# Decoder block on one core: two products of the fourth column pair ahead of the second input half's sums

## The chip, the core and the metric

The kernel runs on 1 core of one Trainium2 chip. The metric is the device time of one execution in microseconds (us). Before the change the median of 3 runs is 2165.49 us (2165.3 to 2165.86). All times of instructions below come from one profiled execution of the same kernel.

## The reference

One decoder layer, in float32, on x of shape (1, 1024 tokens, 1024 features): a gated token mixer, then a squared-ReLU MLP, then a final RMSNorm. The change lies in the first product of the MLP.

```python
h = modulate(rms_norm(x, norm2_g[l]), sh2, sc2)
x = x + g2[:, None, :] * squared_relu_mlp(h, w_ff1[l], w_ff2[l])

def squared_relu_mlp(h, w1, w2):
    return jnp.square(jax.nn.relu(h @ w1)) @ w2      # w1: 1024 x 4096, w2: 4096 x 1024
```

## The kernel before

Activations lie transposed: 8 tiles of 128 features by 1024 tokens. Every float32 operand is split into a high part (a cast on ACT, the scalar engine) and a low part (source minus high part, a subtraction on DVE, the vector engine), and each 128x128 by 128x512 step on PE, the tensor engine, is three matmuls (`mm3`, L210, L212, L214: low weight, low input, high by high).

`ff1` (L2404) computes h @ w1 by a scheme with seven block products in place of eight. The 4096 columns of w1 go in 16 pairs q = 0 to 15 of 2 x 128 columns. The inputs are cut into feature tiles of even and odd number (four of each) and into two halves of 512 tokens. A product is named (q, n); n says which input and weight blocks it takes:

- "11" and "12" take the first token half as it is (`h2h`, `h2l`, split before `ff1` begins) and the pair's weight blocks as they are ("unsummed");
- "s1", "s3", "s2" take sums of input blocks t1, t3, t2 (tiles `xt10h` to `xt13l`, and `xt30`, `xt20` and so on, high and low half of one tile), and weight sums, made on DVE in `fs` by `prep` (L240);
- "s4" takes the second half's odd tiles (`x220h` to `x223l`), "22" the sum t4.

Each product is four steps of `mm3`, 12 matmuls. `prep` makes a product's weights: DVE adds (`fs`, L252, for sums), ACT casts the high part (L257), DVE subtracts for the low part one `prep` later (`flush`, L267). The weight tiles come from a list of slots; the last three tiles called wh and three called wl come back to the list when the product that reads them has been written (`mm`, L281). `post` (L284) takes results out of PSUM: after "11" a copy on ACT (`ft0nsq`, L289); after "s2" two DVE operations (`ft0nsq` L295, `ft0h2t` L296) and one more (`a`, L2360); "22" accumulates on the bank that `ft..h2t` has read, so it has to wait for it. ACT then applies ReLU and the square (L2361, L2362), and `a_sums` (L2377 to L2382) makes the sums that the second MLP product needs.

The order on each engine is the order of the code (`tc.manual_schedule()`); waits between engines are semaphores. At the start of `ff1` the second token half isn't normalised yet: DVE scales its eight tiles (`norm`, L2410), makes t1 (L2432), t3 (L2449), t2 (L2458), t4 (L2475), and ACT and DVE split each sum (`x_split`, L2398 and L2399; L2401 and L2402 for the odd tiles). PE meanwhile computes (0,11), (1,11), (0,12), (1,12), (2,11), (0,s1), (1,s1), (2,12), (0,s3), (1,s3), (0,s2), (1,s2), then the s4 and 22 of pairs 0 and 1, and then pairs 2 to 15 in turn, with (3,11) put between (2,s2) and (2,22). To free its PSUM bank the finished (0,11)+(0,12) is copied aside (L2425, tile `f11`), and later that of pair 2 (L2496).

The raw weights come by `w1_load` (L2326), a DMA of 512 KB on the SP queue, pairs 0 and 1 during the output projection before, pair 2 at its end, pairs 3 and 4 when the input tiles `x1` come free (L2490).

Of the kernel before, what the change touches and what calls it, by code (L numbers as in the profile page):

```python
# [11 lines left out]
F32 = mybir.dt.float32  # L12
# [5 lines left out]
P = 128  # L18
# [122 lines left out]
def block_kernel(ctx, tc, io, stop=None, dbg=None):  # L141
    nc = tc.nc
# [29 lines left out]
    def ps_s(name, shape=(P, 512)):  # L172
        return PS["p"].tile(list(shape), F32, tag="s", bufs=PS["n"], name=name)
# [42 lines left out]
    def wk(w, k):  # L216

        return w[0][:, k * P:(k + 1) * P], w[1][:, k * P:(k + 1) * P]
# [6 lines left out]
    ORDER = ("11", "s1", "s3", "s2", "12", "22", "s4")  # L225
# [3 lines left out]
    class Blocks:  # L229
# [10 lines left out]
        def prep(self, *items):  # L240

            for q, n in items:
                b11, b12 = self.raw[q, 1][:, :512], self.raw[q, 1][:, 512:]
                b21, b22 = self.raw[q, 2][:, :512], self.raw[q, 2][:, 512:]
                if self.low and self.low[:2] == (q, {"s2": "s1", "s4": "s2"}.get(n)):
                    self.flush()
                if n[0] == "s":
                    if n == "s1":
                        self.s[q] = self.sums(f"{self.name}s{q}")
                    src = self.s[q][:, int(n == "s3")]  # L250
                    x, y = {"s1": (b21, b22), "s2": (src, b11), "s3": (b21, b11), "s4": (src, b12)}[n]
                    nc.vector.tensor_add(src, x, y)  # L252
                else:
                    src = {"11": b11, "12": b12, "22": b22}[n]
                kind = self.slots.pop(0)
                t = self.place(kind, f"{self.name}w{q}{n}")
                nc.scalar.copy(t[:, :512], src)  # L257
                self.flush()
                self.low = q, n, t, src
                self.w[q, n] = t, kind  # L260
# [1184 lines left out]
    RGW, n = [], 0  # L1445
# [543 lines left out]
    G = {}  # L1989
# [187 lines left out]
    def r_split(blk, p):  # L2177
        i, hf = 2 * p + int(blk[0]) - 1, int(blk[1]) - 1
        m = G[1, i][:, 512 * hf:512 * hf + 512]
        if blk == "21":  # L2180
            t = A["r1"].tile([P, S], F32R, tag="att", bufs=8, name=f"m{i}{hf}")
            hi, lo = t[:, :512], t[:, 512:]
        else:
            hi, lo = mh(f"mh{i}{hf}"), mh(f"ml{i}{hf}")
        nc.scalar.copy(hi, m)
        nc.vector.tensor_sub(lo, m, fv(hi))
        G["m", i, hf] = hi, lo
# [56 lines left out]
    def norm_acc(x, f, key, pool):  # L2244

        n = x.shape[1]
        if f == 0:
            acc = pool.tile([P, 512], F32, tag="nacc", bufs=2, name=f"acc{key}")[:, :n]
            nc.scalar.activation(acc, x, AF.Square)
            G["acc", key] = acc  # L2250
        else:
            sq = pool.tile([P, 512], F32, tag="nsq", bufs=3, name=f"sq{key}{f}")[:, :n]
            nc.scalar.activation(sq, x, AF.Square)  # L2253
            if key == "nf2" and f == 7:
                G["sq"] = sq
            else:
                (nc.vector if f == 7 else nc.gpsimd).tensor_add(G["acc", key], G["acc", key], sq)  # L2257

    def wo_step(hf, f):
        def body(w):  # L2260
            if hf == 0 and f < 4:
                r_split("12", f)
                r_split("22", f)
            if hf == 0 and 0 < f < 5:
                w1_load((f - 1) % 2, 1 + (f - 1) // 2)
            if (hf, f) in EARLY:
                BF.prep(*EARLY[hf, f])
            if hf == 1 and f in (5, 6):
                w1_load(2, f - 4)
            hs = slice(512 * hf, 512 * hf + 512)  # L2270
            ps = ps_s(f"wo{hf}{f}")
            ks = (0, 2, 4, 6, 1, 3, 5, 7)
            for k in ks:
                mm3([ps], wk(w, k), [G["m", k, hf]], k == 0, k == 7)
            if hf == 1 and f == 0:
                G["rs"] = rstd_rows(G["acc", "n20"], "n20", G["mp"])
            if hf == 1 and f == 1:
                G["rb"] = rstd_bcast(G["rs"], 0, 4, "n20")
            if hf == 1 and 1 < f < 7:
                h2_first(((0, 1), (2,), (3, 4), (5,), (6, 7))[f - 2])  # L2280
            x = G["x1", f][:, hs]
            nc.vector.scalar_tensor_tensor(x, ps, mods[:, G1 + f:G1 + f + 1], x, op0=ALU.mult, op1=ALU.add)
            nc.sync.dma_start(x1_d[f][:, hs], x)
            norm_acc(x, f, f"n2{hf}", G["mp"])
        return body
# [34 lines left out]
    NQ = DFF // 256  # L2320


    NS = 3
    a_d = {t: dram.tile([P, S], F32, name=f"ad{t}") for t in range(8 * NS, 2 * NQ)}
    xs_d = [dram.tile([P, 7, 4, 512], F32, name=f"xsd{c}") for c in range(NS)]
    def w1_load(q, part):  # L2326

        if q < 2:
            t = G["p"].tile([P, 1024], F32, tag="g1", bufs=8, name=f"w1r{q}{part}")
        elif q < 3:  # L2330
            t = wraw.tile([P, 1024], F32, tag="raw", name=f"w1r{q}{part}")
        else:
            t = G["p"].tile([P, 1024], F32, tag="g0", bufs=8, name=f"w1r{q}{part}")
        nc.sync.dma_start(t, io["w_ff1"][2 * q + part - 1])
        BF.raw[q, part] = t
# [10 lines left out]

    def f_temps(name, i):
        t = ("nsq", "h2t")[i]
        return G["mp"].tile([P, 512], F32, tag=t, bufs=3 - i, name=name + t)

    def f_out(q, n, x, y=None):

# [19 lines left out]
    def a_sums(q, part):  # L2372
# [7 lines left out]
        else:  # L2380
# [5 lines left out]
    BF = Blocks("f", X, ["g1"] * 4 + ["att*"] * 4 + ["att"] * 2 + ["att*"] * 2 + ["wh", "wl"] * 3,  # L2386
                lambda kind: kind in ("att", "wh", "wl"), f_place, f_sums, f_temps, f_out)
# [16 lines left out]
    def ff1(ahead):  # L2404
        def t_(k, half):
            return G["x1", k][:, 512 * half:512 * half + 512]
# [14 lines left out]
        BF.prep((2, "s3"), (2, "12"))  # L2421
        BF.mm(0, "12")

        t = G["mp"].tile([P, 512], F32, tag="f11", name="f11")
        nc.scalar.copy(t, BF.ps[0][0])  # L2425
        BF.ps[0][0] = t
        BF.mm(1, "12")
        low = None
        for m in range(4):
            norm(2 * m)  # L2430
# [4 lines left out]
            low = x_split("t1", m, t1, None, "mh", 32)  # L2435
        norm(1)
        low()
        BF.mm(2, "11")
        BF.post(2, "11")
        BF.mm(0, "s1")  # L2440
        BF.mm(1, "s1")
        BF.mm(2, "12")
        lows = []
        for m in range(4):
            if m > 0:
# [6 lines left out]
            low = x_split("t3", m, t3, G["p"], "g1", 8)  # L2452

        def t2(m):
            k = 2 * m + 1
            t = t_(k, 1)
            lows[m]()
            nc.vector.scalar_tensor_tensor(t, t, mods[:, SH2 + k:SH2 + k + 1], t_(2 * m, 0), op0=ALU.add, op1=ALU.add)  # L2458
            return x_split("t2", m, t, G["p"], "g1", 8)

        for m in range(4):
            l = t2(m)
            low()
            low = l
            if m == 0:
                BF.mm(0, "s3")
                BF.mm(1, "s3")
        low()
        BF.mm(0, "s2")
        BF.mm(1, "s2")  # L2470
# [7 lines left out]
        low = t4(0)  # L2478
        BF.post(0, "s2")
        low()  # L2480
        low = t4(1)
        BF.post(1, "s2")
        low()
        low = t4(2)
# [2 lines left out]
        l()  # L2487
        for k in range(NK):
            del G["x1", k]
        for q in (3, 4):  # L2490
            for part in (1, 2):
                w1_load(q, part)
        for q in range(2):
            BF.post(q, "12")
        t = G["mp"].tile([P, 512], F32, tag="f11", name="f11b")
        nc.scalar.copy(t, BF.ps[2][0])  # L2496
        BF.ps[2][0] = t
        sums = [(q, n) for q in range(2, NQ) for n in ORDER if (q, n) not in ((2, "11"), (2, "12"))]
        rest = [(q, n) for q, n in sums if (q, n) != (3, "11")]
        rest.insert(3, (3, "11"))  # L2500
        items = [(q, n) for n in ("s4", "22") for q in range(2)] + rest

        def before(q, n):
            if q > 2 and n == ORDER[0] and q + 2 < NQ:
                for part in (1, 2):
                    w1_load(q + 2, part)
            if q == NQ - 1 and n in ("s2", "12"):
                for f in range(3):
                    x1_load(f + 3 * (n == "12"), x1_d)

        late = {(0, "22"): (0, 0), (2, "s1"): (0, 1), (2, "22"): (1, 0), (2, "s4"): (1, 1), (3, "s1"): (2, 0), (3, "s3"): (2, 1)}
        late.update({(q + 1, n): (q, part) for q in range(3, 4 * NS) for part, n in enumerate(("11", "s1"))})

        def between(q, n):
            if q < 3 and (q, n) in late:
                a_sums(*late[q, n])
            if (q, n) == (2, "22"):
                BF.post(2, "12")
            if (q, n) == (NQ - 1, "22"):
                b_load(1)  # L2520

        def after(q, n):
# [4 lines left out]
            if q == NQ - 1:  # L2527
                second_ahead(n)

        BF.run(items, sums[2:], before, after, lambda q, n: n == "s2" or n == "22" and q < 2,  # L2530
               lambda q: 1 if q == 2 else 9, between)
        b_load(2)
        x1_load(6, x1_d)
        x1_load(7, x1_d)
# [404 lines left out]
```

## Time and profile before

| what | value |
|---|---|
| runs | 2165.3, 2165.49, 2165.86 us |
| the profiled execution's own time | 2165.45 us |
| its span (first to last instruction) | 2163.6 us |
| granted TensorE clock, mean | 0.999 |
| PE busy | 2141.4 us, 99% |
| DVE busy | 1492.1 us, 69% |
| ACT busy | 983.5 us, 45% |
| first and last start of an `ff1` matmul | 1520.1 and 1831.2 us |

A row of the timeline gives the start in us from the span's start, the duration in us, the engine, the line of the kernel, the operation, output and inputs, sizes and count; in brackets the idle time of that engine just before and what ended it. Matmuls overlap: one lasts 0.39 us, and the next starts 0.227 us after it.

### The profile page before, as it was taken

Reading aid. Unit: us, or ns where it says so; the run is one execution under the profiler, and the core shown is the slowest. Engines: PE = TensorE matmul, PEld = TensorE weight load, DVE = VectorE, ACT = ScalarE, POOL = GpSimd, SP = SyncE. Lnnn points to the kernel's source line nnn. Section 1 sums busy time; section 2 is a strip of 40 time slices with the busy share of each in tenths; the row PEclk is TensorE's granted clock in tenths of the full one; section 3 lists DMA queues with packets and bytes.
Section 4 is the critical chain, followed back from the end, with each engine's and each line's share of the span. In section 5 each row is a group of like instructions: output and inputs, shape, how many; then the busy total and the mean of one; then the engine's idle time right before and its main releaser. Section 6 shows DMA issues by size and latency. Waiting matters only on the chain. (4 is left out here: it accounts for less than half of the span.)

```text
span 2163.6 us, 27394 instructions
## 1 busy us (share of the span) xinstructions
PE 2141.4 (99%) x10036; PEld 1782.8 (82%) x10036; DVE 1492.1 (69%) x2320; ACT 983.5 (45%) x1769; POOL 203.2 (9%) x267
## 2 busy tenths in 40 slices
PE   8999999999999999999999999999999999999998
PEld 6888888888888888888888888888778888888887
DVE  6885777777654677666667644777876665977855
ACT  5553322323244566666556635334454455533413
POOL 0001111100001333321110000001000000000003
PEclk9999999999999999999999999999999999999999
DMA  9859998845576655537776366653244435645322
GB/s 383 286 208 301 296 299 248 226 154 202 194 291 241 229 186 180 177 123 213 215 186 188 137 240 221 216 177 129 69 166 161 156 144 195 245 131 175 108 88 78
DMA packets 162931, 425.19 MB, mean 197 GB/s; under 512 B 28261, under 2 KB 56172, under 8 KB 159724
## 3 DMA queue, kind: packets, MB, share of 16 engines
q1 hardware_dynamic: 150456, 374.90, 49.0%
q0 software_dynamic: 9648, 48.24, 10.1%
q8 instruction: 79, 1.29, 0.2%
q10 hardware_dynamic: 2692, 0.30, 0.1%
q14 instruction: 56, 0.46, 0.1%
HBM read 324.13 MB, written 160.32 MB: 224 GB/s over the span
## 5 line engine op out<-in xcount | busy, mean ns | idle before, releaser
L210 PE MATMUL qap<-hh,qaw 128*128 128x512 f32 x264 | 102.7, 389 | 0.0
L212 PE MATMUL qap<-hl,qaw 128*128 128x512 f32 x264 | 102.7, 389 | 0.0
L214 PE MATMUL qap<-hh,qaw 128*128 128x512 f32 x264 | 102.7, 389 | 0.0
L620 POOL TENSOR_TENSOR j<-qk,j 128x512 fp32r<-128x512 f32 x32 | 42.8, 1338 | 400.9 <-ACT j L619 385.5
L2257 POOL TENSOR_TENSOR accnf<-accnf,sqnf 128x256 f32<-128x256 f32 (+1 forms) x18 | 16.6, 923 | 610.0 <-ACT sqnf L2253 610.0
L2361 ACT ACTIVATE a<-a 128x512 f32<-128x512 f32 x48 | 30.3, 631 | 73.7 <-DVE a L2360 73.7
L2569 ACT CAST w2h<-w2s 128x512 fp32r<-128x512 f32 x36 | 22.4, 621 | 78.6 <-DVE w2s L2607 75.7
L214 PEld LDWEIGHTS qap<-hh,qaw 128*128 128x128 f32 x264 | 49.6, 188 | 10.4
L212 PEld LDWEIGHTS qap<-hl,qaw 128*128 128x128 f32 x264 | 49.5, 188 | 10.3
L210 PEld LDWEIGHTS qap<-hh,qaw 128*128 128x128 f32 x264 | 49.5, 188 | 10.3
L267 DVE TENSOR_TENSOR fw<-w1r,fw 128x512 fp32r<-128x512 f32 x48 | 32.9, 688 | 33.6 <-ACT fw L257 33.6
L686 ACT ACTIVATE on<-oT,gnt 128x128 f32<-128x128 f32 x128 | 48.2, 455 | 15.7 <-PE oT L682 15.6
L267 DVE TENSOR_TENSOR qaw<-wa,qaw 128x512 fp32r<-128x512 f32 x66 | 44.0, 686 | 9.6 <-ACT qaw L257 9.6
L2092 DVE TENSOR_TENSOR rwl<-rwl,rwh 128x1024 fp32r<-128x1024 f32 x25 | 30.2, 1220 | 29.1 <-ACT rwh L2122 29.1
L210 PE MATMUL fp<-h2h,fw 128*128 128x512 f32 x128 | 50.0, 390 | 0.0
L1620 ACT ACTIVATE P<-P,ng 128x128 f32<-128x128 f32 (+1 forms) x96 | 41.9, 439 | 17.5 <-DVE ng L1612 17.5
L212 PE MATMUL fp<-h2l,fw 128*128 128x512 f32 x128 | 49.8, 389 | 0.0
L214 PE MATMUL fp<-h2h,fw 128*128 128x512 f32 x128 | 49.8, 389 | 0.0
L210 PE MATMUL roa<-rh,rwl 128*128 128x512 f32 x128 | 49.8, 389 | 0.0
L212 PE MATMUL roa<-rl,rwh 128*128 128x512 f32 x128 | 49.8, 389 | 0.0
L214 PE MATMUL roa<-rh,rwh 128*128 128x512 f32 x128 | 49.8, 389 | 0.0
L656 DVE TENSOR_TENSOR sm<-sm,sT 128x128 f32<-128x128 f32 x32 | 9.2, 288 | 54.6 <-ACT sm L655 54.6
(3092 smaller groups left out, 7214.2 us busy)
## 6 DMA issues: line engine op xcount, KB each, us to landing
v<-vd SPq DMA_DIRECT2D x32, 512.0 KB, 5.1
w1r<-in_w_ff_dram SPq DMA_DIRECT2D x32, 512.0 KB, 4.6
yt<-y POOLq DMA_DIRECT2D x24, 512.0 KB, 7.4
xsd<-as SPq DMA_DIRECT2D x24, 512.0 KB, 2.7
w2r<-in_w_ff2s_dram SPq DMA_DIRECT2D x24, 512.0 KB, 7.0
cossin<-in_w_ada_dram SPq DMA_DIRECT2D x22, 512.0 KB, 3.5
em<-in_w_ada_dram SPq DMA_DIRECT2D x16, 512.0 KB, 10.2
wrvs<-in_w_rv_dram POOLq DMA_DIRECT2D x16, 512.0 KB, 10.1
```

The source lines that it names most:

```text
L210: nc.tensor.matmul(o, wl, xh, start=first, stop=False, skip_group_check=skip)
L212: nc.tensor.matmul(o, wh, xl, start=False, stop=False, skip_group_check=skip)
L214: nc.tensor.matmul(o, wh, xh, start=False, stop=last, skip_group_check=skip)
L267: nc.vector.tensor_sub(t[:, 512:], src, fv(t[:, :512]))
L620: nc.gpsimd.tensor_sub(t[:, 1], src, fv(t[:, 0]))
L656: nc.vector.tensor_add(sm, sm, ps[:, C:2 * C])
L686: nc.scalar.activation(hd["on", h, c // 4][e][:, c % 4 * C:(c % 4 + 1) * C], po[:, e, :], AF.Identity, scale=gnv[0][:, neg + i:neg + i + 1 ...
L1620: nc.scalar.activation(v, v, AF.Exp, bias=ng[:, blk:blk + 1], accum_out=st[:, g, blk, 2 + a:3 + a])
L2092: nc.vector.tensor_sub(lo, fv(lo), fv(hi))
L2257: (nc.vector if f == 7 else nc.gpsimd).tensor_add(G["acc", key], G["acc", key], sq)
L2361: nc.scalar.activation(o, o, AF.Relu)
L2569: nc.scalar.copy(hi, src)
```

## The change

Products (3,11) and (3,12) are moved ahead: (3,11) between (2,12) and (0,s3), (3,12) between (1,s3) and (0,s2). For that, the first half of pair 3's raw weights is loaded during the output projection, into a third buffer of `wraw`, and its two weight tiles are made by `prep` between the other steps. The finished results of pair 1 are copied aside too, as those of pair 0 were, so that a PSUM bank is free for pair 3 (`aside`). The t2 work of the first tile stands behind the rest of the t3 work. After that pairs 2 and 3 are mixed: (2,s1), (2,s3), (2,s2), (3,s1), (2,22), (2,s4), (3,s3), (3,s2), (4,11), (3,22), (3,s4), and then the other pairs in turn, without (4,11).

```diff
@@ Blocks.prep
-                b21, b22 = self.raw[q, 2][:, :512], self.raw[q, 2][:, 512:]
+                low = self.raw[q, 2] if n not in ("11", "12") else self.raw[q, 1]
+                b21, b22 = low[:, :512], low[:, 512:]
@@ norm_acc (and f_temps in the same way)
-            sq = pool.tile([P, 512], F32, tag="nsq", bufs=3, name=f"sq{key}{f}")[:, :n]
+            sq = pool.tile([P, 512], F32, tag="nsq", bufs=4, name=f"sq{key}{f}")[:, :n]
@@ wo_step
+            if hf == 1 and f == 7:
+                w1_load(3, 1)
@@ w1_load
-        elif q < 3:
+        elif q < 3 or (q, part) == (3, 1):
             t = wraw.tile([P, 1024], F32, tag="raw", name=f"w1r{q}{part}")
@@ ff1
         BF.mm(0, "12")
-        t = G["mp"].tile([P, 512], F32, tag="f11", name="f11")
-        nc.scalar.copy(t, BF.ps[0][0])
-        BF.ps[0][0] = t
+        def aside(q):
+            t = G["mp"].tile([P, 512], F32, tag="nacc", bufs=2, name=f"f11{q}")
+            nc.scalar.copy(t, BF.ps[q][0])
+            BF.ps[q][0] = t
+
+        aside(0)
         BF.mm(1, "12")
+        aside(1)
...
         BF.post(2, "11")
+        BF.prep((3, "11"))
         BF.mm(0, "s1")
         BF.mm(1, "s1")
         BF.mm(2, "12")
+        BF.prep((3, "12"))
+        BF.mm(3, "11")
+        BF.post(3, "11")
...
-        for m in range(4):
+        low()
+        low = t2(0)
+        BF.mm(0, "s3")
+        BF.mm(1, "s3")
+        BF.mm(3, "12")
+        for m in range(1, 4):
             l = t2(m)
             low()
             low = l
-            if m == 0:
-                BF.mm(0, "s3")
-                BF.mm(1, "s3")
...
-        rest.insert(3, (3, "11"))
+        sums = [(2, "s1"), (2, "s3"), (2, "s2"), (3, "s1"), (2, "22"), (2, "s4"), (3, "s3"), (3, "s2"), (4, "11"),
+                (3, "22"), (3, "s4")]
```

How the instructions stand now, at three places. The first is ACT's queue in the opening of `ff1`. Before, from the copy aside of pair 0 to the first split of t3 (`xt30`):

```order
L2425 COPY f11_13328<-fp00_13258 128x512
L2398 CAST xt10h_13344<-x1_0_12535 128x512
L2398 CAST xt11h_13350<-x1_2_12537 128x512
L2398 CAST xt12h_13356<-x1_4_12539 128x512
L2398 CAST xt13h_13362<-x1_6_12541 128x512
L289 COPY ft2nsq_13380<-fp20_13367 128x512
L2401 ACTIVATE x220h_13421<-x1_1_12436,mods_73 128x512
L2398 CAST xt30_13425<-x1_0_12535 128x512
```

The same stretch of ACT's queue after the change (fp10 is the PSUM bank of (1,11) and (1,12), fp30 that of (3,11); fw311 and fw312 are the weights of (3,11) and (3,12)):

```order
L2429 COPY f110_13330<-fp00_13260 128x512
L2429 COPY f111_13344<-fp10_13291 128x512
L2401 CAST xt10h_13348<-x1_0_12535 128x512
L2401 CAST xt11h_13354<-x1_2_12537 128x512
L2401 CAST xt12h_13360<-x1_4_12539 128x512
L2401 CAST xt13h_13366<-x1_6_12541 128x512
L290 COPY ft2nsq_13384<-fp20_13371 128x512
L258 CAST fw311_13386<-w1r31_13228 128x512
L258 CAST fw312_13427<-w1r31_13228 128x512
L290 COPY ft3nsq_13443<-fp30_13430 128x512
L2404 ACTIVATE x220h_13445<-x1_1_12436,mods_73 128x512
L2401 CAST xt30_13449<-x1_0_12535 128x512
```

Four instructions have come in: the copy of fp10 ahead of the t1 splits, and two casts and the copy of fp30 ahead of the t3 splits. In the built program the copy of fp10 waits for the last matmul of (1,12), the cast of fw312 for the last matmul of (2,12), whose wl tile it takes over, and the copy of fp30 for the last matmul of (3,11).

The second place is PE's queue behind (2,12). Before, the last step of (2,12) and the first of (0,s3):

```order
L210 MATMUL fp20_13367<-h2h7_13215,fw212_13313 128x512
L212 MATMUL fp20_13367<-h2l7_13216,fw212_13313 128x512
L214 MATMUL fp20_13367<-h2h7_13215,fw212_13313 128x512
L210 MATMUL fp03_13456<-xt30_13425,fw0s3_12832 128x512
L212 MATMUL fp03_13456<-xt30_13425,fw0s3_12832 128x512
```

After the change, the last step of (2,12) and the first of (3,11):

```order
L210 MATMUL fp20_13371<-h2h7_13215,fw212_13315 128x512
L212 MATMUL fp20_13371<-h2l7_13216,fw212_13315 128x512
L214 MATMUL fp20_13371<-h2h7_13215,fw212_13315 128x512
L210 MATMUL fp30_13430<-h2h0_13042,fw311_13386 128x512
L212 MATMUL fp30_13430<-h2l0_13043,fw311_13386 128x512
```

The 12 matmuls of (3,11) stand between (2,12) and (0,s3) now, and those of (3,12) in the same way between (1,s3) and (0,s2).

The third place is DVE's queue ahead of the post of (2,s2) (`ft2nsq`, `ft2h2t`), on which (2,22) waits. Before:

```order
L252 TENSOR_TENSOR fs3_13651<-w1r32_13558,w1r31_13556 128x512
L2381 TENSOR_TENSOR as01_13673<-a1_13531,a0_13530 128x512
L2382 SCALAR_TENSOR_TENSOR as01_13673<-as00_13631,a1_13531 128x512
L267 TENSOR_TENSOR fw3s3_13671<-fs3_13651,fw3s3_13671 128x512
L252 TENSOR_TENSOR fs3_13651<-fs3_13651,w1r31_13556 128x512
L295 TENSOR_TENSOR ft2nsq_13380<-ft2nsq_13380,fp22_13694 128x512
L296 TENSOR_TENSOR ft2h2t_13707<-fp23_13678,ft2nsq_13380 128x512
```

After the change:

```order
L268 TENSOR_TENSOR fw3s3_13689<-fs3_13620,fw3s3_13689 128x512
L253 TENSOR_TENSOR fs3_13620<-fs3_13620,w1r31_13228 128x512
L2384 TENSOR_TENSOR as01_13709<-a1_13568,a0_13567 128x512
L2385 SCALAR_TENSOR_TENSOR as01_13709<-as00_13668,a1_13568 128x512
L268 TENSOR_TENSOR fw3s2_13707<-fs3_13620,fw3s2_13707 128x512
L296 TENSOR_TENSOR ft2nsq_13384<-ft2nsq_13384,fp22_13729 128x512
L297 TENSOR_TENSOR ft2h2t_13742<-fp23_13714,ft2nsq_13384 128x512
```

The weights of (3,s2) are made ahead of this post now, those of (3,11) no longer in this stretch. From the operation behind `ft2h2t` (`a5`) to `ft3nsq`, the post of (3,s2), it is 18 places instead of 20. From `a7`, the operation behind `ft3h2t`, to `ft4nsq` it is 18 in both.

More of the change, by code (lines that the diff above doesn't have):

```diff
@@ L2348, in f_temps @@
         t = ("nsq", "h2t")[i]
-        return G["mp"].tile([P, 512], F32, tag=t, bufs=3 - i, name=name + t)
+        return G["mp"].tile([P, 512], F32, tag=t, bufs=4 - 2 * i, name=name + t)
     def f_out(q, n, x, y=None):
@@ L2489, in ff1 @@
             del G["x1", k]
-        for q in (3, 4):
-            for part in (1, 2):
-                w1_load(q, part)
+        for q, part in ((3, 2), (4, 1), (4, 2)):
+            w1_load(q, part)
         for q in range(2):
             BF.post(q, "12")
[L2495 to L2499, printed above, removed]
-        rest.insert(3, (3, "11"))
-        items = [(q, n) for n in ("s4", "22") for q in range(2)] + rest
+        aside(2)
+        sums = [(2, "s1"), (2, "s3"), (2, "s2"), (3, "s1"), (2, "22"), (2, "s4"), (3, "s3"), (3, "s2"), (4, "11"),
+                (3, "22"), (3, "s4")]
+        sums += [(q, n) for q in range(4, NQ) for n in ORDER if (q, n) != (4, "11")]
+        items = [(q, n) for n in ("s4", "22") for q in range(2)] + sums
         def before(q, n):
-            if q > 2 and n == ORDER[0] and q + 2 < NQ:
+            if q > 2 and n == ("s1" if q < 5 else "11") and q + 2 < NQ:
                 for part in (1, 2):
@@ L2509, in before @@
                     x1_load(f + 3 * (n == "12"), x1_d)
-        late = {(0, "22"): (0, 0), (2, "s1"): (0, 1), (2, "22"): (1, 0), (2, "s4"): (1, 1), (3, "s1"): (2, 0), (3, "s3"): (2, 1)}
-        late.update({(q + 1, n): (q, part) for q in range(3, 4 * NS) for part, n in enumerate(("11", "s1"))})
+        late = {(0, "22"): (0, 0), (2, "s1"): (0, 1), (2, "22"): (1, 0), (2, "s4"): (1, 1), (3, "s3"): (2, 0), (3, "s2"): (2, 1),
+                (4, "s1"): (3, 0), (4, "s3"): (3, 1)}
+        late.update({(q + 1, n): (q, part) for q in range(4, 4 * NS) for part, n in enumerate(("11", "s1"))})
         def between(q, n):
@@ L2516, in between @@
                 a_sums(*late[q, n])
-            if (q, n) == (2, "22"):
-                BF.post(2, "12")
+            if n == "22" and q in (2, 3):
+                BF.post(q, "12")
             if (q, n) == (NQ - 1, "22"):
@@ L2530, in ff1 @@
         BF.run(items, sums[2:], before, after, lambda q, n: n == "s2" or n == "22" and q < 2,
-               lambda q: 1 if q == 2 else 9, between)
+               lambda q: 1 if q in (2, 3) else 9, between)
         b_load(2)
```

## The prediction

> **What bounds the kernel now.** First the busy time of each engine, on the page:
>
> ```profile
> span 2163.6 us, 27394 instructions
> ...
> PE 2141.4 (99%) x10036; PEld 1782.8 (82%) x10036; DVE 1492.1 (69%) x2320; ACT 983.5 (45%) x1769; POOL 203.2 (9%) x267
> ```
>
> PE is the bound over the whole span, and the change takes no matmul away. It can gain only where PE stands still. The view of PE's waits says where, within `ff1`:
>
> ```profile
> PE fp L212 <- DVE xt L2399: 2.0, 2, 1.0
> ...
> PE fp L210 <- DVE ft2h2t L296: 1.3, 1, 1.3
> ...
> PE fp L210 <- DVE ft3h2t L296: 0.6, 1, 0.6
> ...
> PE fp L212 <- DVE xt13l L2399: 0.2, 1, 0.2
> ```
>
> Five waits, 4.1 us in all, every one for DVE. The windows view of the opening (us, busy time of PE, PEld, DVE, ACT, POOL, granted clock, DMA share, GB/s) and of a full pair:
>
> ```profile
> 1536.50:1546.00 9.50, 9.34 (x41) 7.40 (x40) 9.39 (x15) 5.98 (x10) 0.00 (x0) 1.00 0.00 0
> 1546.00:1556.06 10.06, 8.04 (x34) 5.78 (x33) 9.84 (x15) 3.00 (x5) 0.00 (x0) 1.00 0.23 63
> 1599.60:1618.79 19.19, 19.19 (x84) 15.87 (x85) 13.69 (x22) 9.46 (x17) 0.00 (x0) 1.00 0.47 168
> ```
>
> In this opening of `ff1` DVE is the bound, busy 9.39 of 9.50 us and 9.84 of 10.06. So idle time of DVE here is lost for good, while idle PE can be filled. The last row gives PE's price: 84 matmuls (seven products) in 19.19 us, 0.227 each, 2.72 a product.
>
> What a wait costs is read at (2,22), whose first matmul waits:
>
> ```profile
> 1580.71 0.39 PE L214 MATMUL fp<-h2h,fw 128*128 128x512 f32 x1
> 1582.40 0.50 PE L210 MATMUL fp<-xt,fw 128*128 128x512 f32 x1 [1.30 <-DVE ft2h2t L296]
> 1582.73 0.40 PE L212 MATMUL fp<-xt,fw 128*128 128x512 f32 x1
> ```
>
> The start comes 1.69 us after the one before it, in place of 0.227, and the next 0.33 after that: 1.46 + 0.11 = 1.57 lost for a bracket of 1.30. A bracket of w costs w + 0.27. The five together cost 4.1 + 5 x 0.27 = 5.4 us, the most that this change can win.
>
> **The copy of pair 1 (`aside(1)`).** It now heads ACT's queue, ahead of the t1 splits.
>
> ```profile
> 1531.29 0.59 ACT L2425 COPY f<-fp 128x512 f32<-128x512 f32 x1 [1.04 <-PE fp L214]
> 1531.87 0.62 ACT L2398 CAST xt10h<-x 128x512 fp32r<-128x512 f32 x1
> 1533.14 0.69 DVE L2399 TENSOR_TENSOR xt10l<-x,xt10h 128x512 fp32r<-128x512 f32 x1
> 1533.58 0.39 PE L214 MATMUL fp<-h2h,fw 128*128 128x512 f32 x1
> 1538.37 0.68 DVE L2399 TENSOR_TENSOR xt13l<-x,xt13h 128x512 fp32r<-128x512 f32 x1
> 1539.11 0.50 PE L212 MATMUL fp<-xt13l,fw0s 128*128 128x512 f32 x1 [0.16 <-DVE xt13l L2399]
> ```
>
> 1533.58 is the last matmul of (1,12). The copy waits for its end, 1533.97, then takes 0.5 to 0.6 (0.58 between the first two rows); the cast of `xt10h` starts at 34.5 instead of 31.87, and its low part, on DVE 0.65 later, at 35.15 instead of 33.14. DVE stands still for those 2.0 us, `xt13l` comes at 1540.4, and PE's matmul at 1539.11 at 1541.1. **+2.0** here, on a wait that follows again below.
>
> **The weights and the copy of (3,11).** At (2,12) and after:
>
> ```profile
> 1537.76 0.58 ACT L289 COPY ft2nsq<-fp 128x512 f32<-128x512 f32 x1
> 1538.49 0.72 ACT L2401 ACTIVATE x220h<-x,mods 128x512 fp32r<-128x512 f32 x1 [0.15 <-DVE x L2410]
> 1540.35 0.62 ACT L2398 CAST xt<-x 128x512 fp32r<-128x512 f32 x1 [1.14 <-DVE x L2449]
> 1541.68 0.68 DVE L2399 TENSOR_TENSOR xt<-x,xt 128x512 fp32r<-128x512 f32 x1
> 1544.93 0.39 PE L214 MATMUL fp<-h2h,fw 128*128 128x512 f32 x1
> 1546.38 0.75 DVE L2402 SCALAR_TENSOR_TENSOR x220l<-x,mods,x220h 128x512 fp32r<-128x512 f32 x1
> 1547.83 0.68 DVE L2399 TENSOR_TENSOR xt<-x,xt 128x512 fp32r<-128x512 f32 x1
> 1548.57 0.50 PE L212 MATMUL fp<-xt,fw0s 128*128 128x512 f32 x1 [0.98 <-DVE xt L2399]
> 1549.15 0.40 PE L210 MATMUL fp<-xt,fw1s 128*128 128x512 f32 x1
> ```
>
> 1540.35 and 1541.68 are the two halves of `xt30`, 1547.83 the low half of `xt33`; 1544.93 is the last matmul of (2,12), which now comes 2.0 later, at 1546.9. In ACT's queue the cast of `fw312` waits for its end (1547.3), and the copy of `ft3nsq` behind it for (3,11), one product more: last start 1549.66, end 1550.05. Only then come `x220h`, at 1550.6, and the cast of `xt30`, at 1551.25; the low half on DVE at 1551.9 instead of 1541.68, 10.2 later. In DVE's queue all that is left of t3 and t2 stands behind it, so DVE, the bound of this stretch, is idle some 7.5 us. From `xt30`'s low half to `xt33`'s it took 6.15 us; `x220l` and the first t2, 1.45 (1546.38 to 1547.83), stand behind now, so 4.70: `xt33` at 1556.6, its matmul, 0.74 later, at **1557.3** instead of 1548.57.
>
> From there to (0,s2) and (1,s2):
>
> ```profile
> 1553.98 1.46 DVE L2399 TENSOR_TENSOR xt<-x,xt 128x512 fp32r<-128x512 f32 x2
> ...
> 1554.72 0.50 PE L212 MATMUL fp<-xt,fw0s 128*128 128x512 f32 x1 [1.04 <-DVE xt L2399]
> ...
> 1556.06 0.39 PE L210 MATMUL fp<-xt,fw1s 128*128 128x512 f32 x1
> ```
>
> From `x220l` to the low half of `xt22` (1553.98) it was 7.60 with one operation of 0.60 for `xt33`; now it is one for `fw312`'s low part instead, the same 7.60. `x220l` starts at 1557.2, `xt22` at 1564.8, the waiting matmul at 1565.54. PE by itself would be there at 1557.3 + 0.58 + two products + seven matmuls = 1564.9, so (3,12) covers nearly all of that wait, but the whole is late: 1565.54 against 1554.72 is +10.82. Of this, 5.44 are the two products that PE has done ahead. **Net +5.4 up to (1,s2).** The two old waits have not gone, the whole queue has moved.
>
> **(2,22)** waits for `ft2h2t`, with nine products from (1,s2) to it, before and now. These rows, with the times of before (everything now 10.8 later):
>
> ```profile
> 1567.92 0.69 DVE L267 TENSOR_TENSOR fw2s<-fs,fw2s 128x512 fp32r<-128x512 f32 x1 [2.25 <-ACT fw2s L257]
> ...
> 1580.94 0.68 DVE L295 TENSOR_TENSOR ft2nsq<-ft2nsq,fp 128x512 f32<-128x512 f32 x1
> ...
> 1582.38 0.69 DVE L2360 TENSOR_TENSOR a<-ft2h2t,fp 128x512 f32<-128x512 f32 x1
> ```
>
> The same number of DVE operations stands ahead of `ft2nsq`, but the sum for (3,s1) is now made ahead of the 2.25 idle, and the casts for (3,11) and (3,s1) no longer alternate with the ReLUs. Walked step by step from 1567.92, 0.60 a DVE operation and 0.5 to 0.66 an ACT one, `ft2nsq` comes about 1.5 earlier, at 1579.4, and `ft2h2t` ends at 1580.8. PE without a wait is there at 1580.94. Bounds: 0 (no shortening) to the whole wait. I take the whole: **-1.57**.
>
> **(3,22)** waits for `ft3h2t`. Of the products from (2,22) to it, six before, five are left, since (3,12) is done and (4,11) stands for (3,11).
>
> ```profile
> 1598.14 0.68 DVE L295 TENSOR_TENSOR ft3nsq<-ft3nsq,fp 128x512 f32<-128x512 f32 x1
> ...
> 1599.60 0.50 PE L210 MATMUL fp<-xt,fw 128*128 128x512 f32 x1 [0.56 <-DVE ft3h2t L296]
> ```
>
> From `a5` (1582.38) to `ft3nsq` it is 15.76 us for 20 places, 0.788 each with the waits for ACT in them; 18 are left, 14.2. `a5` at 1580.8, `ft3nsq` 1595.0, release of PE (1.46 later, as here) 1596.46. PE without a wait: 1580.94 + 13.60 = 1594.54. So 1.92 + 0.11 = 2.03 lost instead of 0.56 + 0.27 = 0.83: **+1.2**. Bounds: at the 0.60 of an operation that waits for nothing the chain takes 10.9 and the wait is gone, -0.83; with the old 15.76, +2.8. I take 14.2, since the same alternation with ACT is left.
>
> **(4,22)**, six products instead of seven after (3,22):
>
> ```profile
> 1599.58 0.69 DVE L2360 TENSOR_TENSOR a<-ft3h2t,fp 128x512 f32<-128x512 f32 x1
> ...
> 1616.38 0.68 DVE L295 TENSOR_TENSOR ft4nsq<-ft4nsq,fp 128x512 f32<-128x512 f32 x1
> ```
>
> `a7` to `ft4nsq` is 16.80 over 18 places, and it is 18 now. Release of PE after 16.80 + 1.46 - 0.02 = 18.24; PE needs 0.11 + 6 x 2.72 = 16.43, in place of 19.19. 1.81 + 0.11: **+1.9**, bounds 0 and 1.9. From (5,22) on seven products cover the 18.2 again, as in the window of 19.19 above.
>
> **At nothing.** One DMA more stands on the SP queue in the output projection, and three instead of four later:
>
> ```profile
> w1r<-in_w_ff_dram SPq DMA_DIRECT2D x32, 512.0 KB, 4.6
> ```
>
> At 4.6 us it is there long before (2,12) ends, and behind it stands a store that nothing in this stretch waits for; if it delayed the cast, ACT's own wait until 1547 would still hide it. The third buffers and the choice of `low` add no instruction.
>
> **Sum**: 5.4 - 1.57 + 1.2 + 1.9 = +6.9. The profiled execution's own time is 2165.45, the median 2165.49: **2172.4**.
>
> **One price more, the clock.** PE gets thin for 7.5 us, from 1549.9 to 1557.3: three gaps of some 2 us between groups of three matmuls. What a slow restart costs is seen at the start of the kernel:
>
> ```profile
> 11.50 3.47 PE L876 MATMUL av<-wv0wh,hh 128*128 128x512 f32 x8 [1.70 <-ACT hh L413]
> 14.81 2.01 PE L876 MATMUL av<-wv0wh,hl 128*128 128x512 f32 x8
> ```
>
> The first eight matmuls last until 14.81, 3.31, the next eight until 16.66 (14.81 + 2.01 less 0.16 of overlap), 1.85: 1.46 dearer. The granted clock stayed 1.00 in 1546.00 to 1556.06, with gaps of 1 us. I take nothing for it.
>
> [...] No row of before shows PE so thin within `ff1`.
>
> **The rivals.** A, as summed: 2172.4, own range 2170.3 to 2173.9. For it speaks that the ACT waits are in the built order and DVE is 98% busy in that stretch.
>
> B: DVE makes up in the mixed pairs. Its chain has idle time in it (2.25 in one row above), and if it runs at 0.60 the waits at (3,22) and (4,22) go: 5.4 - 1.57 - 0.83 = +3.0, **2168.5**. Against it: that idle time belongs to the alternation with ACT, which the new order keeps.
>
> C: A, and the clock falls in the thin stretch: +1.46, **2173.9**. Against it: gaps of 1 us left the granted clock at 1.00.
>
> D, faster: the queue of ACT isn't held, because the cast of `fw312` finds a free buffer. It decides if that cast starts before about 1539.2, when `ft2nsq` and the cast of `fw311` are done. Then DVE goes on as before, the two products fill both waits of 1.0 and the 0.16, later waits go too, and the whole 5.4 is won: **2160.0**. Against it: the cast's wait for (2,12) and the copy's for (3,11) stand in the built program. That the change doesn't act at all is excluded by the order of PE's queue.
>
> **How the numbers follow.** A 0.69, B 0.17, C 0.09, D 0.05. The measurement tells 0.2%, 4.33 us, from no change: 2161.2 to 2169.8. A and C are slower; B lies within; D is split, 0.02 faster, 0.03 within if some of the later waits stay. Faster 0.02, same 0.20, slower 0.78. The range takes in A, C and B: 2168.2 to 2174.2.
>
> **What would show it.** In the trace of after: on ACT the cast of `fw312` ended by (2,12) and the copy of `ft3nsq` by (3,11); on DVE an idle of about 7.5 ahead of `xt30`'s low half, and 2.0 ahead of `xt10`'s; on PE (0,s3)'s four steps spread over 1550 to 1557, (1,s2) at 1566.9 (B, C too); no wait at (2,22), brackets of about 1.8 and 1.6 at (3,22) and (4,22) (none in B); in C a granted clock under 1.00 behind 1557. The forecast is wrong if `xt30`'s cast starts before 1545 (D), or if DVE's chains to `ft3nsq` and `ft4nsq` are under 12.1 and 15.0 us (PE's five and six products less the 1.46).

## The result

2173.02 us median of 6 runs (2172.14 to 2175.7) against 2165.49 (2164.95 to 2166.6): the ratio is 1.0032, 95% interval 1.0022 to 1.0042. The kernel became slower by 7.5 us; the forecast was 2172.4.

### The profile after

The profiled execution's own time is 2174.12 us, its span 2172.3. PE's waits, those within `ff1` (us in total, times, longest):

```profile
PE fp L210 <- ACT xt L2401: 1.8, 1, 1.8
PE fp L210 <- DVE ft3h2t L297: 1.7, 1, 1.7
...
PE fp L212 <- DVE xt L2402: 1.2, 3, 0.6
PE fp L210 <- DVE ft4h2t L297: 1.2, 1, 1.2
...
PE fp L212 <- DVE xt12l L2402: 1.0, 1, 1.0
```

Before there were the five waits that the prediction lists, 4.1 us, and a sixth that it left out, at (15,22), near the end of `ff1`:

```profile
PE fp L210 <- DVE ft15h2t L296: 0.2, 1, 0.2
```

Now there are nine, 7.5 us (two of 0.3 for `xt11l` and `xt13l` are not in the rows above). Those at (2,22) and (15,22) have gone, that at (3,22) has grown from 0.6 to 1.7, and one of 1.2 at (4,22) is new. One is for ACT. Its queue, the instructions that came in and those behind them (the brackets hold the idle time before and what ended it):

```profile
1536.12 0.59 ACT L2429 COPY f<-fp 128x512 f32<-128x512 f32 x1 [2.13 <-PE fp L214]
1536.60 0.62 ACT L2401 CAST xt10h<-x 128x512 fp32r<-128x512 f32 x1
...
1549.51 0.62 ACT L258 CAST fw<-w1r 128x512 fp32r<-128x512 f32 x1 [6.54 <-PE fp L214]
1552.18 0.58 ACT L290 COPY ft3nsq<-fp 128x512 f32<-128x512 f32 x1 [2.05 <-PE fp L214]
1552.66 0.72 ACT L2404 ACTIVATE x220h<-x,mods 128x512 fp32r<-128x512 f32 x1
1553.29 0.61 ACT L2401 CAST xt<-x 128x512 fp32r<-128x512 f32 x1
```

The copy of pair 1 (1536.12), the cast of `fw312` (1549.51) and the copy of `ft3nsq` (1552.18) each wait for PE, and the splits stand behind them. On DVE the two low halves that wait for those splits, `xt10` and `xt30`:

```profile
1537.25 0.69 DVE L2402 TENSOR_TENSOR xt10l<-x,xt10h 128x512 fp32r<-128x512 f32 x1 [1.93 <-ACT xt10h L2401]
...
1553.92 0.69 DVE L2402 TENSOR_TENSOR xt<-x,xt 128x512 fp32r<-128x512 f32 x1 [7.44 <-ACT xt L2401]
```

DVE, the bound of this stretch before, stands still for 1.93 and 7.44 us. On PE, the first step of (0,s3), the wait for `xt31`, the last two matmuls of that product, the start of (1,s3), (1,s2), and the start of (2,22), (3,22) and (4,22), each of which needs a post:

```profile
1553.94 0.50 PE L210 MATMUL fp<-xt,fw0s 128*128 128x512 f32 x1 [1.80 <-ACT xt L2401]
...
1556.71 0.79 PE L212 MATMUL fp<-xt,fw0s 128*128 128x512 f32 x1 [0.62 <-DVE xt L2402]
...
1560.21 0.63 PE L212 MATMUL fp<-xt,fw0s 128*128 128x512 f32 x1
1560.64 0.63 PE L214 MATMUL fp<-xt,fw0s 128*128 128x512 f32 x1
1561.07 0.63 PE L210 MATMUL fp<-xt,fw1s 128*128 128x512 f32 x1
...
1569.60 0.39 PE L210 MATMUL fp<-xt,fw1s 128*128 128x512 f32 x1
...
1594.47 0.39 PE L210 MATMUL fp<-xt,fw 128*128 128x512 f32 x1
...
1609.94 0.50 PE L210 MATMUL fp<-xt,fw 128*128 128x512 f32 x1 [1.70 <-DVE ft3h2t L297]
...
1627.79 0.50 PE L210 MATMUL fp<-xt,fw 128*128 128x512 f32 x1 [1.23 <-DVE ft4h2t L297]
```

Matmuls last 0.63 in place of 0.39, and start 0.43 after one another in place of 0.227. The windows view (us, busy time of PE, PEld, DVE, ACT, POOL, granted clock, DMA share, GB/s) shows why:

```profile
1552.00:1554.00 2.00, 0.20 (x2) 0.06 (x1) 0.08 (x1) 1.82 (x4) 0.00 (x0) 1.00 0.00 0
1554.00:1555.00 1.00, 0.78 (x2) 0.43 (x3) 1.00 (x2) 1.00 (x2) 0.00 (x0) 0.98 0.00 0
1555.00:1561.00 6.00, 4.98 (x11) 2.95 (x10) 5.81 (x10) 2.74 (x6) 0.00 (x0) 0.50 0.00 0
1561.00:1563.00 2.00, 2.00 (x8) 1.60 (x7) 1.97 (x4) 0.58 (x1) 0.00 (x0) 0.80 0.00 0
```

After two microseconds with almost nothing on PE the granted clock fell; narrower windows put the stretch at 0.50 from 1554.95 to 1561.78.

Where the time went, by the starts of PE's products, counted from the first matmul of `ff1` (1520.09 before, 1522.21 after). "Later, net" is the difference less the products that PE has done ahead at that point (2.72 each):

| point | before | after | later, net | the step | forecast of the step |
|---|---|---|---|---|---|
| (1,s2) | 35.97 | 47.39 | +5.98 (two ahead) | +5.98 | +5.4 |
| (2,22) | 62.31 | 72.26 | +4.51 (two) | -1.47 | -1.57 |
| (3,22) | 79.51 | 87.73 | +5.50 (one) | +0.99 | +1.2 |
| (4,22) | 98.70 | 105.58 | +6.88 (none) | +1.38 | +1.9 |

The table takes each step at the first matmul of a product. Behind a wait the second matmul is slow too (0.33 after the first in place of 0.227), and these 0.11 us fall into the next row. Put to the wait that they belong to, the last three steps are -1.58, +1.10 and +1.49, and the sum is +7.0. It stays +7.0 up to the last product with `h2h`; at (15,22) the wait of before (0.15, with its restart 0.42) is gone, so over the whole of `ff1` it is +6.6. The two profiled executions are 8.67 apart, since that of after also lost 2.1 ahead of `ff1`:

```profile
1058.33 0.70 PE L210 MATMUL gate<-hh,raw_8961l 128*128 128x512 f32 x2 [2.35 <-DVE raw_8961l L201]
```

This wait lies in a stage that the change does not touch. Of the nine experiments' profiles one has it, with 1.1 us (both_later), and that of before has not; so it is taken to belong to the execution and not to the change.

### The profile page after: what moved, and what is told of

The parts are those of the page before. It is cut to its first block, busy times and chain, and to the rows that moved or that the text cites. A ratio compares the mean times of both kernels' runs of the same rounds, so it can differ in the third digit from the quotient of the medians.

```text
span 2172.3 us, 27388 instructions
## 1 busy us (share of the span) xinstructions
PE 2145.1 (99%) x10036; PEld 1785.0 (82%) x10036; DVE 1491.0 (69%) x2320; ACT 983.5 (45%) x1770; POOL 201.9 (9%) x267
```

## The experiments

Theory Q (queue): the time is lost because three ACT instructions that wait for PE stand ahead of the splits that DVE, the bound, needs. Rival C (clock): most of it is the half-rate stretch. Rival W (work): DVE's added operations and the later order cost it, wherever ACT's instructions stand. Besides the medians of whole runs (before, beside them on the same chip: 2165.4 to 2165.7), one measure from the profiles is used that leaves out what happens in other stages: the **ff1 stretch**, from the first to the last start of a low-weight matmul on `h2h`. For the kernel before and after (the view of that tile; count, shortest, median and longest ns, first and last start):

```profile
L210 PE MATMUL fp<-h2h,fw x128: 389/389/478, 1520.1 to 1827.6; 128*128 128x512 f32 x128
```
```profile
L210 PE MATMUL fp<-h2h,fw x128: 389/389/486, 1522.2 to 1836.7; 128*128 128x512 f32 x128
```

307.5 and 314.5, +7.0. The stretch ends ahead of (15,22) (`ff1` itself goes on to the s4 of pair 15, whose last matmul starts at 1833.89 before, not at 1831.2). So the wait for `ft15h2t` is not in it: none is listed for the change, copy_later, weights_later, fill_nine and both_later_sums, 0.2 to 0.3 in the kernel before, clock_fill and post_later, 0.5 in borrow and mix_alone, 0.9 in both_later. The change and the nine experiments:

| kernel | median, us (runs) | ratio to before, 95% | ff1 stretch against before |
|---|---|---|---|
| the change | 2173.02 (6) | 1.0032 (1.0022 to 1.0042) | +7.0 |
| copy_later | 2170.48 (11) | 1.0022 (1.0013 to 1.0030) | +5.4 |
| post_later | 2169.63 (11) | 1.0018 (1.0009 to 1.0027) | +3.9 |
| weights_later | 2166.66 (11) | 1.0005 (0.9997 to 1.0014) | +0.2 |
| both_later | 2163.93 (11) | 0.9992 (0.9984 to 1.0001) | -1.8 |
| clock_fill | 2172.96 (8) | 1.0032 (1.0021 to 1.0043) | +6.4 |
| fill_nine | 2171.83 (1) | | +6.5 |
| both_later_sums | 2162.23 (11) | 0.9983 (0.9974 to 0.9993) | -3.8 |
| borrow | 2160.50 (8) | 0.9973 (0.9963 to 0.9984) | -5.3 |
| mix_alone | 2163.16 (11) | 0.9988 (0.9979 to 0.9997) | -2.6 |

### copy_later: the copy of pair 1 behind the t1 splits

```diff
         BF.mm(1, "12")
-        aside(1)
...
         norm(1)
         low()
+        aside(1)
         BF.mm(2, "11")
```

> The changed kernel with one ACT copy moved: pair 1's finished results are copied aside behind the four t1 casts instead of ahead of them. Queue theory (the loss comes from ACT instructions that wait for PE ahead of the splits): the idle 1.93 us of DVE ahead of xt10's low half is gone, (2,12) ends 2.0 us earlier, and all behind it with it: about 2170.5, 2.0 below the changed kernel's lower runs plus their spread (2170 to 2171.5). Clock theory (most of the loss is the half-rate stretch after the thin one): PE is as thin as before, 2172 to 2173.

2170.48, 2.5 below the changed kernel; the stretch is 1.6 shorter. DVE's idle time ahead of `xt10l` is gone and PE no longer waits in (0,s1). Of the 2.0 expected the stretch lost 0.4 within (1,s3): up to the start of that product it was 1.97 ahead of the change, and from there to (1,s2) it took 8.90 us instead of 8.53. The clock fell later here, about 3.6 us after the end of (3,11) instead of 2.8, and slowed four matmuls of (1,s3) instead of two (the next one starts 0.35 to 0.43 us after each of them, in place of 0.227).

### weights_later: the cast of fw312 and the copy of ft3nsq behind the t3 splits

```diff
         BF.mm(2, "12")
-        BF.prep((3, "12"))
+        BF.flush()
         BF.mm(3, "11")
-        BF.post(3, "11")
...
         low()
+        BF.prep((3, "12"))
+        BF.post(3, "11")
         low = t2(0)
```

> The changed kernel with the cast of fw312 and the copy of ft3nsq moved in ACT's queue behind the four casts of t3; the order of PE is unchanged. Queue theory: the 7.4 us idle of DVE ahead of xt30's low half is gone, (3,11) covers what is left of the DVE stretch, only the 2.0 us of the t1 splits stay: (1,s2) 0.7 earlier than in the kernel before (without the moved products), then -1.6 at (2,22), +1.1 at (3,22), +1.5 at (4,22): 2165.8 (2165 to 2167). Rival, DVE's own added work (two more low parts, 1.2 us) and the later order cost it: no better than 2170. Clock theory: the same time as the queue theory, since PE isn't thin then.

2166.66, stretch +0.2 (2165.8 and +0.3 expected). PE's order is that of the change, DVE does the same operations, and nearly 7 us have gone. That refutes W. PE's waits in `ff1`:

```profile
PE fp L210 <- DVE ft3h2t L297: 1.7, 1, 1.7
PE fp L210 <- DVE ft4h2t L297: 1.2, 1, 1.2
PE fp L212 <- DVE xt12l L2402: 1.0, 1, 1.0
PE fp L212 <- DVE xt13l L2402: 0.3, 1, 0.3
PE fp L212 <- DVE xt11l L2402: 0.3, 1, 0.3
```

(0,s3) and (0,s2) don't wait at all: the two early products cover DVE's stretch, as they were meant to, once ACT's queue doesn't hold DVE. Left are the waits of the t1 splits and those of the mixed pairs.

### post_later: the copy of ft3nsq alone behind the t3 splits

```diff
         BF.mm(3, "11")
-        BF.post(3, "11")
...
         low()
+        BF.post(3, "11")
         low = t2(0)
```

> The changed kernel with the copy of ft3nsq alone moved behind the four casts of t3; the cast of fw312 still waits for (2,12) ahead of them. Queue theory: ACT is free again about 2.7 us earlier, when the cast of fw312 is done and not when (3,11) is, so DVE's idle time ahead of xt30's low half falls from 7.4 to about 4.8 us, PE goes on from (3,11) to (0,s3) without the gap of 1.8 us, the clock stays at 1.00, and the total is 2169.3 (2168.5 to 2170.5). If the copy's wait alone held the queue, it would be near 2165.5 to 2167, as weights_later; if the cast's alone did, near 2172 to 2173.

2169.63, stretch +3.9. So the hold is made of both, the cast's wait for (2,12) and the copy's for (3,11) behind it. DVE at `xt30`'s low half:

```profile
1548.81 0.69 DVE L2402 TENSOR_TENSOR xt<-x,xt 128x512 fp32r<-128x512 f32 x1 [4.82 <-ACT xt L2401]
```

4.82 instead of 7.44: the 2.6 between them is about one product (2.72). The granted clock stayed at 1.00.

### both_later: the edits of copy_later and weights_later together

> Both moves together. Queue theory: DVE never stands still in the opening, the two products fill the 0.16 and the two 1.0 us waits: 3.0 us below the kernel before up to (1,s2), then -1.6 +1.1 +1.5: 2163.5 (2162.5 to 2164.5), with waits left only at (3,22) and (4,22). Rival (the added DVE work is the loss): not below 2165.5.

2163.93, stretch -1.8. DVE's only idle time from the t1 splits to the post of (0,s2) is 1.44 us at that post, for PE. The waits that are left stand where the expectation has them, in the mixed pairs, and one that it doesn't have is 0.9 for `ft15h2t` at the end of `ff1`.

### clock_fill and fill_nine: matmuls in the gaps

Fifteen matmuls more than in the change (clock_fill), or only the nine ahead of (0,s3) (fill_nine). They add nothing to the output.

```diff
         low = t2(0)
-        BF.mm(0, "s3")
+        BF.ps[1][3] = ps_s("fp13")
+        tf = BF.w[3, "11"][0]
+
+        def fill(n):
+            for i in range(n):
+                mm3([BF.ps[1][3]], (tf[:, i * P:i * P + P], tf[:, 512 + i * P:512 + i * P + P]), [X["11", i]], i == 0, i == n - 1, True)
+
+        fill(3)
+        for m in range(4):
+            BF.mm(0, "s3", range(m, m + 1))
+            if m < 2:
+                fill(1)
         BF.mm(1, "s3")
```

> The changed kernel with 15 more matmuls on PE in its thin stretch: nine between (3,11) and (0,s3), three each behind the first two steps of (0,s3), written to a PSUM bank that (1,s3) then starts anew, so they add nothing to the output. Queue theory: the granted clock stays at 1.00, the steps of (0,s3) still come every 2.05 us as DVE delivers them, (1,s2) starts some 0.6 us earlier than in the changed kernel, the total 0 to 0.8 below it: 2171.8 to 2173. Clock theory: the half-rate stretch is most of the loss: 2167 to 2168.

> clock_fill with only the nine matmuls between (3,11) and (0,s3). If the clock falls for the one gap of 1.8 us ahead of (0,s3), it stays at 1.00 now. If it falls for the thin stretch as a whole, the gaps between the steps of (0,s3) bring it down, later than in the changed kernel. The time in both cases 2171.5 to 2173.5, since DVE sets the pace.

clock_fill: 2172.96, stretch +6.4, 0.6 under the change. The granted clock is 1.00 in every window from 1515 to 1640 us, which holds the whole opening of `ff1`, and the loss stays: that refutes C as the account of it. (1,s2) comes +5.5 late, net, against the +5.98 of the change. At the end of `ff1` even this is gone, since clock_fill waits at (15,22) and the change doesn't: over the whole of `ff1` both are +6.6, and the medians are alike. That the fall is no accident of one execution is seen in the mean granted clock of every run: 0.997 in five of the change's six and 0.998 in one, 0.998 or 0.999 in all eight of clock_fill.

In fill_nine, of which there is a single execution, the clock stayed at 1.00 too, in the thin stretch itself:

```profile
1552.00:1554.00 2.00, 1.26 (x5) 0.48 (x3) 1.97 (x4) 1.65 (x4) 0.00 (x0) 1.00 0.00 0
1554.00:1557.00 3.00, 1.34 (x5) 0.82 (x6) 2.88 (x5) 1.92 (x3) 0.00 (x0) 1.00 0.00 0
```

PE is busy 1.34 of 3.00 us there, with gaps of 1.09 and 1.08 us. Without the fill, the gap of 1.80 with 0.20 busy in 2.00 us was followed by 0.50. That it is the gap that decides doesn't follow from this; the last section comes back to it.

### both_later_sums: DVE's chain in the mixed pairs

both_later, and:

```diff
-        late = {(0, "22"): (0, 0), (2, "s1"): (0, 1), (2, "22"): (1, 0), (2, "s4"): (1, 1), (3, "s3"): (2, 0), (3, "s2"): (2, 1),
-                (4, "s1"): (3, 0), (4, "s3"): (3, 1)}
-        late.update({(q + 1, n): (q, part) for q in range(4, 4 * NS) for part, n in enumerate(("11", "s1"))})
+        late = {(0, "22"): (0, 0), (2, "s1"): (0, 1), (2, "22"): (1, 0), (2, "s4"): (1, 1), (3, "s2"): (2, 0), (4, "11"): (2, 1),
+                (4, "s3"): (3, 0), (4, "s2"): (3, 1)}
+        late.update({(q + 1, n): (q, part) for q in range(4, 4 * NS) for part, n in enumerate(("s1", "s3"))})
```

> Both moves of ACT's instructions, and the sums that the second MLP product needs (a_sums) one product later from pair 2 on, so that the sum that waits for ACT no longer stands ahead of ft3nsq on DVE. If the wait at (3,22) is DVE's chain from a5 to ft3nsq (14.3 us for PE's 13.6), the chain is 12.3 us and the wait of 1.7 goes, that at (4,22) stays: 2161.9 (2161 to 2163), 2.0 below both_later. Rival, the wait comes from the products that are missing and DVE only shifts it to (4,22): as both_later, 2163.9.

2162.23, stretch -3.8, 2.0 under both_later. In `ff1` PE waits 1.2 us at (4,22), as before this edit, and 0.2 for `xt13l`. So it was DVE's chain that made the wait at (3,22): shortened, it is covered by the five products that are left.

### borrow: seven products in every pair

both_later_sums, and:

```diff
-        sums += [(q, n) for q in range(4, NQ) for n in ORDER if (q, n) != (4, "11")]
+        for q in range(4, NQ):
+            own = [(q, "11")] if q > 13 else []
+            sums += own + [(q, "s1"), (q, "s3"), (q, "s2"), (q, "12")]
+            sums += ([(q + 1, "11")] if q < 13 else []) + [(q, "22"), (q, "s4")]
...
-            if q > 2 and n == ("s1" if q < 5 else "11") and q + 2 < NQ:
+            if q > 2 and n == "s1" and q + 2 < NQ:
```

> both_later_sums, and the 11 product of the next pair taken ahead in every pair up to pair 13 instead of in pair 3 alone, so that seven products again stand between (3,22) and (4,22). If that wait is PE's six products against DVE's chain, it goes: 2160.4 (2159.5 to 2161.5). Rival (the pairs behind inherit the wait, or the later sums make a new one): not below 2162.

2160.50 (2160.09 to 2161.35), 0.27% under the kernel before on the same chip (2165.43). What PE still waits for in `ff1`:

```profile
PE fp L210 <- DVE ft15h2t L297: 0.5, 1, 0.5
```

And two windows of the opening:

```profile
1536.00:1545.60 9.60, 9.47 (x42) 7.50 (x42) 9.46 (x16) 6.21 (x11) 0.00 (x0) 1.00 0.00 1
1545.60:1558.00 12.40, 12.40 (x56) 10.27 (x55) 11.30 (x17) 5.41 (x9) 0.00 (x0) 1.00 0.22 75
```

In the second row PE is busy all of 12.40 us, where it was busy 8.04 of 10.06 in the window of before that ends at (1,s2).

### mix_alone: only the later order, from the kernel before

The opening is that of before. Behind pair 3 the order is that of borrow (its diff), and before that:

```diff
-        rest = [(q, n) for q, n in sums if (q, n) != (3, "11")]
-        rest.insert(3, (3, "11"))
+        sums = [(2, "s1"), (2, "s3"), (2, "s2"), (3, "11"), (3, "s1"), (2, "22"), (2, "s4"), (3, "s3"), (3, "s2"),
+                (3, "12"), (4, "11"), (3, "22"), (3, "s4")]
...
```

> The kernel before, its opening untouched, (3,11) and (3,12) not moved ahead; only the later order is mixed as in borrow, with the sums one product later. The three waits of the opening stay (3.0 us with their restarts), those at (2,22) and (3,22) go (1.6 and 0.8): 2163.1 (2162 to 2164.5). If it comes below 2161.5, moving the two products ahead brings nothing by itself.

2163.16, stretch -2.6. The difference to borrow, 2.7 us, is what the early products bring when ACT's queue is left free: the two waits of 1.0 us in the opening stay here. The rest of borrow's gain, some 2.3 us, comes from the later order and does not need the two products moved ahead.

## Why the prediction was right, by its steps

- **The copy of pair 1, +2.0.** DVE stood still for 1.93. PE paid in three waits of (0,s1), 0.3, 1.0 and 0.3, where the text had the whole in the last of them, that for `xt13l`; the matmul behind it came 1.99 later, as forecast (from the start of `ff1` 21.01 us instead of 19.02). copy_later took the idle time away.
- **The cast and the copy ahead of the t3 splits.** Forecast: DVE idle 7.5, measured 7.44; a start of `x220h` at 1550.6, measured 1552.66 less the 2.12 by which `ff1` began later, 1550.54. weights_later and post_later show that it is these two, in series.
- **Net +5.4 up to (1,s2)** measured +5.98. The 0.6 is the clock, for which the sum took nothing: in clock_fill, with the clock at 1.00, the step is +5.5. This is the step that was wrong. The clock did fall, for which C had a chance of 0.09, to a granted 0.50 for 6.83 us. Up to (1,s2) it cost 0.5 to 0.6 and not C's 1.46: DVE set the pace of (0,s3), so that the slow matmuls filled gaps, and the wait of about 0.6 for `xt22` that the sum held went away in exchange (in clock_fill it is there, 0.43 by its bracket). The 1.46 was read from rows of before (11.50 to 16.66 us) in which the granted clock is 1.00, and no run shows it as the price of a fall.
- **(2,22), -1.57** measured -1.58 with the restart (-1.47 in the table): the wait is gone.
- **(3,22), +1.2** measured +1.10 (+0.99 in the table). DVE's chain:

```profile
1594.19 0.69 DVE L2363 TENSOR_TENSOR a<-ft2h2t,fp 128x512 f32<-128x512 f32 x1
...
1608.48 0.68 DVE L296 TENSOR_TENSOR ft3nsq<-ft3nsq,fp 128x512 f32<-128x512 f32 x1
1609.19 0.69 DVE L297 TENSOR_TENSOR ft3h2t<-fp,ft3nsq 128x512 f32<-128x512 f32 x1
1609.92 0.69 DVE L2363 TENSOR_TENSOR a<-ft3h2t,fp 128x512 f32<-128x512 f32 x1
...
1626.33 0.68 DVE L296 TENSOR_TENSOR ft4nsq<-ft4nsq,fp 128x512 f32<-128x512 f32 x1
```

From `a5` (1594.19) to `ft3nsq` 14.29 (forecast 14.2).
- **(4,22), +1.9** measured +1.49 (+1.38 in the table). From `a7` (1609.92) to `ft4nsq` 16.41 instead of the 16.80 taken over from before: the number of places was the same, but the waits for ACT in them, by their brackets, were 5.1 us instead of 5.4. The term was too large by 0.4, which cancels most of the clock.
- **Rival B** (no waits at (3,22) and (4,22)) is refuted by the brackets of 1.70 and 1.23. **D** (ACT not held) did not happen. both_later, which is the change with the queue free, shows that half of it holds: the two products fill the waits of the opening. Its price doesn't: both_later takes 2163.93 and not 2160.0, since the waits at (3,22) and (4,22) are there all the same. borrow comes near that price, 2160.50, but by two changes more.

That the total came so close to 2172.4 is partly chance: the two misses, 0.6 and 0.4, had opposite signs. The list of PE's waits also left out the one at (15,22), 0.42 with its restart, which then came and went from kernel to kernel without being forecast.

## What to carry to other kernels

Work put ahead of a wait to fill it brings its own preparation, and that stands in some engine's queue. Before counting the filled gap, follow each new instruction in its in-order queue: what it waits for, and which instructions behind it the bounding engine needs. Here 5.4 us of product were put in the right place on PE, and two ACT instructions of 1.2 us together held DVE for 7.4 us. Issued behind the splits, the same instructions held nothing up, and the two products gained 2.7 us (borrow against mix_alone).

## What the runs showed of the hardware

In the change the granted clock fell to 0.50 at 1554.95, 2.8 us after the end of PE's last matmul of (3,11), and stayed there for 6.83 us. In copy_later it fell about 3.6 us after the end of that matmul and was back at 1.00 about 6.8 us later: its mean is 0.58 from 1551 to 1552 us, 0.50 from 1552 to 1557 and 0.75 from 1557 to 1559. In both PE had stood still for 1.80 us there.

The length of the gap alone does not decide it. The wait in `gate` shown above is longer, 2.35 us, in the same execution, and the clock stayed at 1.00. Nor does the time that PE is busy around the gap alone. Two stretches of 3.00 us of the change, the one that ended with the fall, and one around the gap of 2.35 with the 8 us about it:

```profile
1551.95:1554.95 3.00, 0.97 (x3) 0.47 (x3) 1.03 (x2) 2.77 (x5) 0.00 (x0) 1.00 0.00 0
1055.98:1058.98 3.00, 0.65 (x4) 0.59 (x4) 2.10 (x3) 1.90 (x3) 0.00 (x0) 1.00 0.90 92
1054.00:1062.00 8.00, 5.65 (x31) 4.62 (x30) 5.96 (x14) 5.92 (x11) 0.51 (x1) 1.00 0.55 64
```

PE is busy for 0.97 us in the first, which the fall followed, and for 0.65 in the second, which none followed. What decides it, these runs do not show.
